# A decoder layer on one core: a gate row turned before its store, two compression layers in sequence, two heads' scores in one matmul

## The chip, the cores and the metric

The kernel runs on one core of a Trainium2 chip. The metric is the device time of one execution in microseconds. TensorE (PE) multiplies, VectorE (DVE) and ScalarE (ACT) work on elements, GpSimd (POOL) does a few powers and issues part of the DMAs, SyncE (SP) issues the weight loads.

## The reference, cut to what matters

One layer for 256 tokens of width 2048: a modulated norm, an input projection, two groups of attention heads, an output projection with gate 1, and then a product-key expert layer with gate 2. The modulation vectors are rows of `silu(c) @ w_ada + b_ada`. In the first group of heads, keys and values are also compressed: 32 tokens become one by a two-layer network, and the queries score the 15 compressed keys of their head group.

```python
def nsa_compress(k, pe, w1, w2, idx):
    ...
    out = jax.nn.gelu(blk @ w1) @ w2
...
Kc = nsa_compress(kc, pe_k, ck_w1, ck_w2, cmp_idx)
Vc = nsa_compress(vc, pe_v, cv_w1, cv_w2, cmp_idx)
...
s_c = jnp.einsum('bgrqd,bgnd->bgrqn', qi, Kc).astype(F32) * scale - slopes * d_c.astype(F32)
...
x = x + gate1 * (jnp.concatenate([o_nsa, o_ret], axis=-1) @ w_out[l])
```

## The kernel before, in words

The kernel has a front stage (everything up to the second norm, about the first 570 us) and an expert stage behind it, in which the expert tables u and v stream through TensorE. The change lies in the front, but for a call that is written differently.

Every weight block of the front arrives as a tile `raw` of 1 MB, in a ring of four buffers, issued by SP in program order. ACT casts it to `whi` and DVE forms the rest `wlo` (line 158, two halves per block, two buffers each); TensorE multiplies with both. Beside this stream run the 96 blocks of `w_ada` (`adaT`): DVE multiplies each with the row `crow` and sums it into one column of `modc` (line 198). The function `background` deals them out between the projection's blocks, `todo` holds their order: rows 1 and 0, then row 2 (gate 1), 4, 3 and 5 (gate 2).

A scheduler with a simulated timeline orders the instructions of each engine, except those that `keep_in_program_order` pins; each engine then works through its queue in that order. Tiles with the same tag share the buffers of a pool; in PSUM the tags A, S, T and O have two banks each.

The places that the change touches:

- Compression (lines 467 to 503). For keys, then values: DVE writes `blk` (one buffer) by eight additions, TensorE multiplies the 16 blocks of `w1` with it into `psc`, ACT takes the Gelu into `hid`. The second layer of the keys (`psk`, copied to `KcT`) stands ahead of the first layer of the values; then `hpad` and `psv` give the values in block-diagonal form (`BD`).
- Attention. For each of two pairs of head groups (`gp`), window and selected scores `sc` are formed, with exponentials `pr`, transposes `pT` and products `po`; between them the pairs of the projection's second half (`d_pair`, tile `psD`) and of the retention's values (`n_tile`, tile `psN`) run. At the end of each `gp`, the compressed scores `scc` (line 570) are formed, for each half `hf` of the 128 partitions by itself, as a query tile's 64 rows times 15 keys.
- Gate 1 (lines 200 to 209). `gate_store(2)` writes `modc[:, 2, :]`, 128 partitions of 16 numbers, as a row of 2048 numbers to DRAM, on POOL's queue. `row_load` reads the row back into all 128 partitions (1 MB) as `g1`. The output projection's first tile is multiplied with it (`xg`, line 716).
- Gate 2's row was already turned on TensorE and stored as 16 rows of 128 numbers, written out in place.

Of the kernel before, what the change touches and what calls it, by code (L numbers as in the profile page):

```python
# [9 lines left out]
F32 = mybir.dt.float32  # L10
# [6 lines left out]
AF = mybir.ActivationFunctionType  # L17
# [3 lines left out]
P = 128  # L21
S = 256
D = 2048
KB = D // P
# [3 lines left out]
NCMP = 15  # L28
# [87 lines left out]
def body(ctx, tc, a, out, dbg=None, stop=None):  # L116
    nc = tc.nc
# [3 lines left out]
    def dump(name, ap):  # L121
        if name in dbg:
            nc.sync.dma_start(dbg[name], ap)
# [47 lines left out]
    dram = ctx.enter_context(tc.tile_pool(name="dram", bufs=1, space=bass.MemoryType.DRAM))  # L171
# [5 lines left out]
    modc = base.tile([P, 6, KB], F32, name="modc")  # L177
# [19 lines left out]
        r = load(a["adaT"][j, k])  # L197
        nc.vector.scalar_tensor_tensor(r, r, 1.0, crow, op0=OP.mult, op1=OP.mult, accum_out=modc[:, j, k:k + 1])  # L198

    def gate_store(j):  # L200

        row = dram.tile([1, D], F32, name=f"row{j}")
        with nc.allow_non_contiguous_dma(reason="one row of 2048 numbers"):
            nc.gpsimd.dma_start(row.rearrange("o (k p) -> p (o k)", p=P), modc[:, j, :])
        return row

    def row_load(dst, row):

        nc.gpsimd.dma_start(dst, bass.AP(tensor=row.tensor, offset=row.offset, ap=[[0, P], [1, D]]))
# [68 lines left out]
    with ExitStack() as fctx:  # L278
        strm.append((fctx.enter_context(tc.tile_pool(name="strm", bufs=1)), dict(raw=4, whi=2, wlo=2)))
        fp = fctx.enter_context(tc.tile_pool(name="front", bufs=1))  # L280
# [28 lines left out]
        pp = fctx.enter_context(tc.tile_pool(name="fpsum", bufs=2, space=PS))  # L309
# [83 lines left out]
        for k in range(KB):  # L393
# [43 lines left out]
        qts = [xT[:, i, :] for i in range(8)]  # L437
# [27 lines left out]
        gate4 = gate.rearrange("p t (h b) -> p t h b", b=3)  # L465


        KcT = fp.tile([P, 4, NCMP], F32, name="KcT")
        BD = fp.tile([P, 4, 4, 64], F32, name="BD")
        nc.gpsimd.memset(BD, 0.0)  # L470
        pad = fp.tile([P, 4, 4, 32], F32, name="hpad", tag="tmp2", bufs=3)
        nc.gpsimd.memset(pad, 0.0)
        for kv in range(2):
            w1 = load(a["cw1"][kv].rearrange("p k e -> p (k e)"))
            psc = pp.tile([P, 4, NCMP], F32, name="psc", tag="S")
            view = kT2[:, 2 * kv:2 * kv + 2].rearrange("p a h (n e) -> p e (a h) n", e=8)
            blk = fp.tile([P, 16, 4, NCMP], F32, name="blk", bufs=1)
            for q in range(2):
                pe = csm[:, kv * 16 + 8 * q:kv * 16 + 8 * q + 8]
                for g in range(4):  # L480
                    nc.vector.tensor_add(blk[:, 8 * q:8 * q + 8, g, :], view[:, :, g, q:q + NCMP],
                                         pe[:, :, None].to_broadcast([P, 8, NCMP]))
            for pb in range(16):
                nc.tensor.matmul(psc, w1[:, pb * P:(pb + 1) * P], blk[:, pb], start=pb == 0, stop=pb == 15)
            hid = fp.tile([P, 4, NCMP], F32, name="hid", bufs=2)
            nc.scalar.activation(hid, psc, AF.Gelu_apprx_tanh)
            if kv == 0:
                w2 = csm[:, 32:96]
                psk = pp.tile([P, 4, NCMP], F32, name="psk", tag="S")
                w2d = fp.tile([P, 2, 64], F32, name="w2d")  # L490
                nc.vector.tensor_copy(w2d[:, 0, :], w2)
                nc.vector.tensor_copy(w2d[:, 1, :], w2)
                nc.tensor.matmul(psk, w2d.rearrange("p a d -> p (a d)"), hid, start=True, stop=True)
                nc.vector.tensor_copy(KcT, psk)
            else:
                for r in range(4):
                    nc.vector.tensor_copy(pad[:, :, r, 0:NCMP], hid)
                psv = pp.tile([P, 4, 64], F32, name="psv", tag="S")
                for g in range(4):
                    nc.tensor.matmul(psv[:, g, :], pad[:, g].rearrange("p r n -> p (r n)"), csm[:, 96:160],  # L500
                                     start=True, stop=True)
                for r in range(4):
                    nc.vector.tensor_copy(BD[32 * r:32 * r + 32, :, r, :], psv[32 * r:32 * r + 32, :, :])
        dump("KcT", KcT)
        dump("BD", BD)
        dump("gate", gate)

# [10 lines left out]
        for gp in range(2):  # L518
            o = fp.tile([P, 2, 8, 64], F32, name="onsa", bufs=1)
            ppad = fp.tile([P, 2, 8, 32], F32, name=f"ppad{gp}")  # L520
            nc.gpsimd.memset(ppad, 0.0)
            for r in range(4):
# [5 lines left out]
                for hf in range(2):  # L528
                    g = 2 * gp + hf
                    h = 4 * g + r  # L530
                    hs = slice(hf * 64, hf * 64 + 64)
# [30 lines left out]
                for hf in range(2):  # L562
                    nc.vector.tensor_add(o[:, :, hf * 4 + r, :], tmp[:, hf, :, 0, :], tmp[:, hf, :, 1, :])

            scs = [pp.tile([P, 2, 4, 16], F32, name="scc", tag="S") for _ in range(2)]
            for hf in range(2):
                hs = slice(hf * 64, hf * 64 + 64)
                for r in range(4):
                    for tt in range(2):
                        nc.tensor.matmul(scs[hf][:, tt, r, 0:NCMP], qts[gp * 4 + r][hs, tt * 128:(tt + 1) * 128],  # L570
                                         KcT[hs, 2 * gp + hf, :], start=True, stop=True)
            pv = ppad[:, :, :, 0:NCMP]
            den = fp.tile([P, 2, 8], F32, name="denc", bufs=1)
            mx = fp.tile([P, 2, 8], F32, name="mxc", bufs=1)
            bc = lambda x: x[:, :, None].to_broadcast([P, 8, NCMP])
            for tt in range(2):
                for hf in range(2):
                    nc.vector.tensor_add(pv[:, tt, 4 * hf:4 * hf + 4], scs[hf][:, tt, :, 0:NCMP],
                                         ncmp[:, tt, 8 * gp + 4 * hf:8 * gp + 4 * hf + 4, :])
                nc.vector.tensor_reduce(mx[:, tt, :], pv[:, tt], axis=AX.X, op=OP.min)  # L580
                nc.vector.tensor_sub(pv[:, tt], pv[:, tt], bc(mx[:, tt, :]))
                nc.scalar.activation(pv[:, tt], pv[:, tt], AF.Exp, scale=-1.0)
                nc.vector.reduce_sum(den[:, tt, :], pv[:, tt], axis=AX.X)
                nc.vector.tensor_mul(pv[:, tt], pv[:, tt], cval[:, tt, None, :].to_broadcast([P, 8, NCMP]))
# [19 lines left out]
            of = o.rearrange("p t h d -> p (t h) d")  # L604
# [96 lines left out]
        g1 = None  # L701
        x2d = dram.tile([P, 2, D], F32, name="x2d")
        for q in range(4):
            sl = slice(q * 512, (q + 1) * 512)
            ps = n_tile(q, "woutN", "AS"[q % 2], "out")
            if q == 0:
                while any(j == 2 for j, _ in todo):
                    background(1)
                g1 = fp.tile([P, D], F32, name="g1", tag="cT")
                row_load(g1, gate_store(2))  # L710
            if q == 3:
                background(len(todo))
            with tc.high_priority(offset=100 if q == 3 else 0):
                for tt in range(2):
                    t = fp.tile([P, 512], F32, name="xg", tag="tmp2", bufs=3)
                    nc.vector.tensor_mul(t, ps[tt], g1[:, sl])
                    nc.vector.tensor_add(x2[:, tt, sl], x2[:, tt, sl], t)
                    sq = fp.tile([P, 512], F32, name="sq2", tag="tmp2", bufs=3)
                    nc.scalar.activation(sq, x2[:, tt, sl], AF.Square, accum_out=ss[:, tt, q:q + 1])
                    nc.gpsimd.dma_start(x2d[:, tt, sl], x2[:, tt, sl])  # L720
# [23 lines left out]
    with ExitStack() as gctx:  # L744
        strm.append((gctx.enter_context(tc.tile_pool(name="strm2", bufs=1, reuse_waits="tile")), dict(raw=5, whi=3, wlo=2)))
        gp_ = gctx.enter_context(tc.tile_pool(name="peer", bufs=1, reuse_waits="tile"))
        ident = gp_.tile([P, P], F32, name="ident2")
# [387 lines left out]
        for i in range(16):  # L1135
            ps = first[i] if i < 2 else t_block(up, wq(i), bank("A"), dst=early if i == 2 else None)
# [134 lines left out]

        nc.vector.tensor_add(modc[:, 5, :], modc[:, 5, :], b_col[:, 5, :])
        nc.vector.tensor_scalar(modc[:, 5, :], modc[:, 5, :], 1.0 / GSC, None, op0=OP.mult)
        ps = up.tile([P, 512], F32, name="psh", tag=bank("S"))
        nc.tensor.transpose(ps[0:KB, 0:P], modc[:, 5, :], ident)
        r5 = gp_.tile([KB, P], F32, name="row5t", tag="ge", bufs=3)
        nc.scalar.copy(r5, ps[0:KB, 0:P])
        row5 = dram.tile([1, D], F32, name="row5")
        nc.gpsimd.dma_start(row5.rearrange("o (k p) -> (o k) p", p=P), r5)
        for _ in range(2):  # L1280
            x_tile(gp_)

# [13 lines left out]
def build(tc, a, out, dbg=None):  # L1296
    with ExitStack() as ctx:
        body(ctx, tc, a, out, dbg)
# [17 lines left out]
```

## Time and profile before

| | |
|---|---|
| median of 3 runs | 1890.0 us (1884.99 to 1891.03) |
| the profiled execution | 1895.85 us, its span 1894.1 us |
| PE busy | 1816.1 us, 96% |
| DVE busy | 1479.9 us, 78% |
| DMA moved | 652.93 MB, mean 345 GB/s |
| matmuls of `psN` (L452) | 172.8 us with whi, 104.4 us with wlo |

Busy time is summed over the whole span; a busy PE can still be slow, since short matmuls and a lowered clock count as busy. Times in rows of the timeline are microseconds from the span's start: start, duration, engine, line, operation, then in brackets how long the engine stood idle and for what. One fp32 matmul appears as two records in the profile.

### The profile page before, as it was taken

To read this page: it belongs to the slowest core of one execution; us is meant where nothing else is said; L and a number is where in the kernel's file an instruction comes from. 1 tells how busy PE (TensorE), PEld (TensorE's weight loads), DVE (VectorE), ACT (ScalarE), POOL (GpSimd) and SP (SyncE) were. 2 spreads that over 40 slices of the span, in tenths; PEclk is the share of its full clock that TensorE was granted. 3 is DMA by queue.
4 is the path that set the end of the run, shared out by engine and by line. 5 is a ranking of instruction groups with operands and counts; after the bars stand their busy time and mean duration, and the time that the engine had idled before them with its cause. 6 is when DMAs were issued, how large, how long until landed. Compare 5 with 4: busy or idle time off the path is not lost.

```text
span 1894.1 us, 28604 instructions
## 1 busy us (share of the span) xinstructions
PE 1816.1 (96%) x11303; PEld 1589.3 (84%) x11303; DVE 1479.9 (78%) x2333; ACT 708.7 (37%) x1279; POOL 379.5 (20%) x256
## 2 busy tenths in 40 slices
PE   5899999999997999999999999999999999999995
PEld 4899878788786899999997777779999997777773
DVE  7988877879788998778388999974455559888875
ACT  3444453625434422011035545541111114555552
POOL 1000001002001002111124444421111125544210
PEclk9999899989998999999999999999999999999998
DMA  8989876879887979999889999989989979999981
GB/s 350 388 323 373 309 274 231 311 258 349 298 321 276 339 278 342 424 395 355 356 320 406 422 417 413 416 337 425 367 330 355 366 301 421 422 413 387 383 294 45
DMA packets 94473, 652.93 MB, mean 345 GB/s; under 512 B 11409, under 2 KB 11617, under 8 KB 18433
## 3 DMA queue, kind: packets, MB, share of 16 engines
q1 hardware_dynamic: 66818, 467.78, 64.2%
q0 software_dynamic: 27520, 183.32, 24.2%
q8 instruction: 89, 1.46, 0.3%
q14 instruction: 46, 0.38, 0.1%
HBM read 644.97 MB, written 4.22 MB: 343 GB/s over the span
## 4 chain that ended last, share of the span: by engine, by line
PE 84%; DVE 9%; DMA 3%; issue 2%; ACT 1%; POOL 0%; SPq 0%; ACTq 0%; POOLq 0%; DVEq 0%
PE acc L964 31%; PE psU L1062 28%; PE psN L452 8%; PE psD L353 3%; DMA raw<-in_adaT 2%; PE bkB L353 2%; PE psA L236 2%; DVE raw L198 2%; DVE wlo L158 2%; PE pg L1047 1%; PE bkC L353 1%; PE bvB L405 1%; PE psA L237 1%; DMA raw<-in_winA 1%; PE pT L548 1%
## 5 line engine op out<-in xcount | busy, mean ns | idle before, releaser
L1062 PE MATMUL psU<-xT,raw 128*128 128x160 f32 x4096 | 569.9, 300 | 0.0
L1062 PEld LDWEIGHTS psU<-xT,raw 128*128 128x128 f32 x4096 | 558.3, 190 | 0.5
L964 PE MATMUL acc<-whi,cc 128*128 128x512 f32 x1512 | 367.8, 391 | 0.0
L964 PEld LDWEIGHTS acc<-whi,cc 128*128 128x128 f32 x1512 | 283.8, 188 | 68.9
L947 DVE TENSOR_TENSOR wlo<-raw,whi 128x2048 fp32r<-128x2048 f32 x126 | 288.2, 2288 | 63.6 <-issue 58.5
L964 PE MATMUL acc<-wlo,cc 128*128 128x512 f32 x1008 | 252.5, 391 | 0.6 <-DVE wlo L947 0.6
L946 ACT CAST whi<-raw 128x2048 fp32r<-128x2048 f32 x126 | 240.7, 1911 | 6.5 <-DMA raw<-in_v 6.5
L157 ACT CAST whi<-raw 128x1024 fp32r<-128x1024 f32 (+1 forms) x174 | 168.5, 1018 | 187.3 <-PE psN L452 43.8
L198 DVE SCALAR_TENSOR_TENSOR raw<-raw,crow 128x2048 f32<-128x2048 f32 x96 | 219.2, 2284 | 23.3 <-DMA raw<-in_adaT 23.2
L158 DVE TENSOR_TENSOR wlo<-raw,whi 128x1024 fp32r<-128x1024 f32 (+1 forms) x174 | 200.9, 1181 | 30.8 <-ACT whi L157 28.2
L964 PEld LDWEIGHTS acc<-wlo,cc 128*128 128x128 f32 x1008 | 162.0, 161 | 61.6 <-DVE wlo L947 1.3
L452 PE MATMUL psN<-whi,act 128*128 128x512 f32 x512 | 172.8, 414 | 1.3 <-ACT whi L157 1.1
L1068 DVE TENSOR_TENSOR X<-X,ge 128x160 f32<-128x160 f32 (+19 forms) x94 | 25.8, 276 | 165.3 <-ACT ge L1067 158.0
L1064 ACT ACTIVATE X<-psU 128x160 f32<-128x160 f32 (+19 forms) x102 | 25.6, 253 | 306.3 <-PE psU L1062 298.3
L452 PEld LDWEIGHTS psN<-whi,act 128*128 128x128 f32 x512 | 97.7, 194 | 26.9 <-issue 3.0
L452 PE MATMUL psN<-wlo,act 128*128 128x512 f32 x256 | 104.4, 410 | 3.6 <-DVE wlo L158 3.6
L941 ACT CAST cc<-X 128x192 fp32r<-128x192 f32 x128 | 44.8, 353 | 157.0 <-PE acc L964 155.9
L236 PE MATMUL psA<-act,whi 128*128 128x512 f32 x240 | 87.9, 407 | 3.2 <-ACT whi L157 3.2
L803 POOL DMA_INDIRECT rows<-in_urow,sx x32 | 71.8, 2244 | 91.6 <-DVE rows L844 76.3
L803 POOL DMA_INDIRECT s<-in_urow,sx x26 | 57.5, 2213 | 134.6 <-DVE s L844 101.9
L803 POOL DMA_INDIRECT xT<-in_v,sx x21 | 60.7, 2889 | 93.0 <-DVE cc L942 63.2
L844 DVE SCALAR_TENSOR_TENSOR rows<-rows,h2t 128x2048 f32<-128x2048 f32 x32 | 73.1, 2286 | 3.5 <-DMA rows<-in_urow,sx 3.5
(350 smaller groups left out, 2550.9 us busy)
## 6 DMA issues: line engine op xcount, KB each, us to landing
raw<-in_u SPq DMA_DIRECT2D x128, 1024.0 KB
raw<-in_v SPq DMA_DIRECT2D x128, 1024.0 KB
raw<-in_adaT SPq DMA_DIRECT2D x96, 1024.0 KB
raw<-in_winN SPq DMA_DIRECT2D x16, 1024.0 KB
raw<-in_woutN SPq DMA_DIRECT2D x16, 1024.0 KB
raw<-in_wqT SPq DMA_DIRECT2D x16, 1024.0 KB
raw<-in_winB SPq DMA_DIRECT2D x16, 832.0 KB
raw<-in_winD SPq DMA_DIRECT2D x12, 1024.0 KB
```

What stands on the lines that cost most here:

```text
L157: nc.scalar.copy(hi[:, sl], r[:, sl])
L158: nc.vector.tensor_sub(lo[:, sl], r[:, sl], hi[:, sl].bitcast(F32))
L198: nc.vector.scalar_tensor_tensor(r, r, 1.0, crow, op0=OP.mult, op1=OP.mult, accum_out=modc[:, j, k:k + 1])
L236: nc.tensor.matmul(p_, hi[:, sl], act[:, k], start=k == 0, stop=False, skip_group_check=True)
L353: nc.tensor.matmul(bank[:, b, :], x[:, w], y[:, k, :], start=k == k0 and n == 0 and first, stop=k == k1 - 1 and n == 2, skip_group_check=True)
L452: nc.tensor.matmul(ps[tt], x[:, k, ts_], y[:, w], start=k == 0 and j == 0, stop=k == KB - 1 and j == 2)
L803: pin(nc.gpsimd.indirect_dma_start(out=r, out_offset=None, in_=src, in_offset=bass.IndirectOffsetOnAxis(ap=o, axis=0)))
L844: pin(nc.vector.scalar_tensor_tensor(r, r, 1.0, h, op0=OP.mult, op1=OP.mult, accum_out=d[:, e:e + 1]))
L946: inorder(nc.scalar.copy(hi, r))
L947: nc.vector.tensor_sub(lo, r, hi.bitcast(F32))
L964: nc.tensor.matmul(acc[c][0:m], x, w[:, c[1] * 512:(c[1] + 1) * 512], start=jj == 0 and n == 0, stop=jj == HALF - 1 and n == 2 - c[0], ski ...
L1062: nc.tensor.matmul(ps, w[:, k * P:(k + 1) * P], xT[:, k, 0:TU], start=k == 0, stop=k == KB - 1)
```

## The change

Three edits. `gate_store` now takes a PSUM tile and a small SBUF tile: TensorE transposes the 16 columns of `modc`, ACT copies the result, and POOL stores 16 rows of 128 numbers; gate 2 calls the same function. In the compression both first layers are formed before the key's second layer, and the last matmul of the values' first layer and the key's second layer are pinned in that order. The compressed keys are kept as `Kc`, with 32 columns per pair of head groups: the first 16 hold one group's keys in the upper 64 partitions, the last 16 the other group's in the lower 64, and zeros elsewhere. One matmul over all 128 partitions so gives the scores of both halves.

```diff
-    def gate_store(j):
+    def gate_store(j, ps, ident, t):
         row = dram.tile([1, D], F32, name=f"row{j}")
-        with nc.allow_non_contiguous_dma(reason="one row of 2048 numbers"):
-            nc.gpsimd.dma_start(row.rearrange("o (k p) -> p (o k)", p=P), modc[:, j, :])
+        nc.tensor.transpose(ps, modc[:, j, :], ident)
+        nc.scalar.copy(t, ps)
+        nc.gpsimd.dma_start(row.rearrange("o (k p) -> (o k) p", p=P), t)
         return row
...
-        KcT = fp.tile([P, 4, NCMP], F32, name="KcT")
+        Kc = fp.tile([P, 2, 2, 16], F32, name="Kc")
+        nc.gpsimd.memset(Kc, 0.0)
...
             for pb in range(16):
-                nc.tensor.matmul(psc, w1[:, pb * P:(pb + 1) * P], blk[:, pb], start=pb == 0, stop=pb == 15)
-            hid = fp.tile([P, 4, NCMP], F32, name="hid", bufs=2)
-            nc.scalar.activation(hid, psc, AF.Gelu_apprx_tanh)
-            if kv == 0:
-                ...
-                nc.tensor.matmul(psk, w2d.rearrange("p a d -> p (a d)"), hid, start=True, stop=True)
-                nc.vector.tensor_copy(KcT, psk)
-            else:
-                ...
+                i = nc.tensor.matmul(psc, w1[:, pb * P:(pb + 1) * P], blk[:, pb], start=pb == 0, stop=pb == 15)
+            hids.append(fp.tile([P, 4, NCMP], F32, name="hid", bufs=2))
+            nc.scalar.activation(hids[-1], psc, AF.Gelu_apprx_tanh)
+        tc.keep_in_program_order(i)
...
+        tc.keep_in_program_order(nc.tensor.matmul(psk, w2d.rearrange("p a d -> p (a d)"), hids[0], start=True, stop=True))
+        for gp in range(2):
+            for hf in range(2):
+                hs = slice(hf * 64, hf * 64 + 64)
+                nc.vector.tensor_copy(Kc[hs, gp, hf, 0:NCMP], psk[hs, 2 * gp + hf, :])
...
-            scs = [pp.tile([P, 2, 4, 16], F32, name="scc", tag="S") for _ in range(2)]
-            for hf in range(2):
-                hs = slice(hf * 64, hf * 64 + 64)
-                for r in range(4):
-                    for tt in range(2):
-                        nc.tensor.matmul(scs[hf][:, tt, r, 0:NCMP], qts[gp * 4 + r][hs, tt * 128:(tt + 1) * 128],
-                                         KcT[hs, 2 * gp + hf, :], start=True, stop=True)
+            scs = pp.tile([P, 2, 4, 2, 16], F32, name="scc", tag="S")
+            for r in range(4):
+                for tt in range(2):
+                    nc.tensor.matmul(scs[:, tt, r].rearrange("p h n -> p (h n)"), qts[gp * 4 + r][:, tt * 128:(tt + 1) * 128],
+                                     Kc[:, gp].rearrange("p h n -> p (h n)"), start=True, stop=True)
...
-                row_load(g1, gate_store(2))
+                row_load(g1, gate_store(2, pp.tile([P, P], F32, name="psg1", tag="T")[0:KB, :], ident,
+                                        fp.tile([KB, P], F32, name="row2t")))
...
-        ps = up.tile([P, 512], F32, name="psh", tag=bank("S"))
-        nc.tensor.transpose(ps[0:KB, 0:P], modc[:, 5, :], ident)
-        ...
-        nc.gpsimd.dma_start(row5.rearrange("o (k p) -> (o k) p", p=P), r5)
+        row5 = gate_store(5, up.tile([P, 512], F32, name="psh", tag=bank("S"))[0:KB, 0:P], ident,
+                          gp_.tile([KB, P], F32, name="row5t", tag="ge", bufs=3))
```

The scheduler re-deals the neighbours of these instructions. On TensorE at the compression, before (the line numbers of the changed kernel are a few higher than those of the kernel before):

```order
L353 MATMUL psD<-act,wlo 128x256
L484 MATMUL psc<-blk,raw 128x60 x16
L353 MATMUL psD<-act,whi 128x256 x2
L493 MATMUL psk<-hid,w2d 128x60
L484 MATMUL psc<-blk,raw 128x60 x16
```

and in the changed kernel:

```order
L354 MATMUL psD<-act,wlo 128x256
L487 MATMUL psc<-blk,raw 128x60 x16
L354 MATMUL psD<-act,whi 128x256 x2
L487 MATMUL psc<-blk,raw 128x60 x16
L496 MATMUL psk<-hid,w2d 128x60
```

The second run of `psc` has moved ahead of `psk`.

On POOL's queue, before, with `row` the stored gate row, `g` the loaded one, `nal` and `dec` masks, `msn` and `brs` powers for norms, `x2d` the stored result:

```order
L533 DMA nal<-in_nali 128x384 x9
L204 DMA row_4435<-modc 128x16x1
L220 TENSOR_TENSOR msn<-msn,mhalf 128x16
L533 DMA nal<-in_nali 128x384 x3
L642 DMA dec<-in_dec 128x384 x8
L220 TENSOR_TENSOR msn<-msn,mhalf 128x16
L220 TENSOR_TENSOR brs<-brs,mhalf 128x2 x2
L209 DMA g_4434<-row_4435 128x2048
L220 TENSOR_TENSOR brs<-brs,mhalf 128x2 x6
L720 DMA x2d<-xT 128x512 x8
```

and in the changed kernel:

```order
L537 DMA nal<-in_nali 128x384 x9
L221 TENSOR_TENSOR msn<-msn,mhalf 128x16
L537 DMA nal<-in_nali 128x384 x3
L644 DMA dec<-in_dec 128x384 x8
L221 TENSOR_TENSOR msn<-msn,mhalf 128x16
L221 TENSOR_TENSOR brs<-brs,mhalf 128x2 x8
L205 DMA row_4423<-row2t 16x128
L210 DMA g_4420<-row_4423 128x2048
L723 DMA x2d<-xT 128x512 x8
```

Store and load have both moved behind the last `brs`, one directly behind the other.

On DVE, where the loaded row is first used (`xg`), with `wlo` the splits for the next weight blocks and `modc` the adaT sums, before:

```order
L198 SCALAR_TENSOR_TENSOR raw,modc<-raw,crow 128x2048
L676 TENSOR_TENSOR act<-oT,act 128x256
L716 TENSOR_TENSOR xg<-psN,g_4434 128x512
L717 TENSOR_TENSOR xT<-xT,xg 128x512
L158 TENSOR_TENSOR wlo<-raw,whi 128x1024
L716 TENSOR_TENSOR xg<-psN,g_4434 128x512
L158 TENSOR_TENSOR wlo<-raw,whi 128x1024
```

and in the changed kernel:

```order
L678 TENSOR_TENSOR act<-oT,act 128x256
L198 SCALAR_TENSOR_TENSOR raw,modc<-raw,crow 128x2048
L158 TENSOR_TENSOR wlo<-raw,whi 128x1024 x3
L719 TENSOR_TENSOR xg<-psN,g_4420 128x512
L158 TENSOR_TENSOR wlo<-raw,whi 128x1024
L720 TENSOR_TENSOR xT<-xT,xg 128x512
L719 TENSOR_TENSOR xg<-psN,g_4420 128x512
L720 TENSOR_TENSOR xT<-xT,xg 128x512
L198 SCALAR_TENSOR_TENSOR raw,modc<-raw,crow 128x2048
```

Three halves of `wlo` now stand ahead of the first `xg`, and one between the two.

More of the change, by code (lines that the diff above doesn't have):

```diff
@@ L472, in body @@
         nc.gpsimd.memset(pad, 0.0)
+        hids = []
         for kv in range(2):
@@ L483, in body @@
             for pb in range(16):
-                nc.tensor.matmul(psc, w1[:, pb * P:(pb + 1) * P], blk[:, pb], start=pb == 0, stop=pb == 15)
-            hid = fp.tile([P, 4, NCMP], F32, name="hid", bufs=2)
-            nc.scalar.activation(hid, psc, AF.Gelu_apprx_tanh)
-            if kv == 0:
[L488 to L493, printed above, removed]
-                nc.vector.tensor_copy(KcT, psk)
-            else:
-                for r in range(4):
[L497 to L503, printed above, removed]
@@ L504, in body @@
-        dump("KcT", KcT)
+                i = nc.tensor.matmul(psc, w1[:, pb * P:(pb + 1) * P], blk[:, pb], start=pb == 0, stop=pb == 15)
+            hids.append(fp.tile([P, 4, NCMP], F32, name="hid", bufs=2))
+            nc.scalar.activation(hids[-1], psc, AF.Gelu_apprx_tanh)
+        tc.keep_in_program_order(i)
+        w2 = csm[:, 32:96]
+        psk = pp.tile([P, 4, NCMP], F32, name="psk", tag="S")
+        w2d = fp.tile([P, 2, 64], F32, name="w2d")
+        nc.vector.tensor_copy(w2d[:, 0, :], w2)
@@ new lines, in body @@
+        nc.vector.tensor_copy(w2d[:, 1, :], w2)
+        tc.keep_in_program_order(nc.tensor.matmul(psk, w2d.rearrange("p a d -> p (a d)"), hids[0], start=True, stop=True))
[4 more added lines that the diff above has]
+        for r in range(4):
+            nc.vector.tensor_copy(pad[:, :, r, 0:NCMP], hids[1])
+        psv = pp.tile([P, 4, 64], F32, name="psv", tag="S")
@@ L505, in body @@
+        for g in range(4):
+            nc.tensor.matmul(psv[:, g, :], pad[:, g].rearrange("p r n -> p (r n)"), csm[:, 96:160],
+                             start=True, stop=True)
+        for r in range(4):
+            nc.vector.tensor_copy(BD[32 * r:32 * r + 32, :, r, :], psv[32 * r:32 * r + 32, :, :])
         dump("BD", BD)
@@ L563, in body @@
                     nc.vector.tensor_add(o[:, :, hf * 4 + r, :], tmp[:, hf, :, 0, :], tmp[:, hf, :, 1, :])
-            scs = [pp.tile([P, 2, 4, 16], F32, name="scc", tag="S") for _ in range(2)]
-            for hf in range(2):
-                hs = slice(hf * 64, hf * 64 + 64)
-                for r in range(4):
-                    for tt in range(2):
-                        nc.tensor.matmul(scs[hf][:, tt, r, 0:NCMP], qts[gp * 4 + r][hs, tt * 128:(tt + 1) * 128],
-                                         KcT[hs, 2 * gp + hf, :], start=True, stop=True)
+            scs = pp.tile([P, 2, 4, 2, 16], F32, name="scc", tag="S")
+            for r in range(4):
+                for tt in range(2):
+                    nc.tensor.matmul(scs[:, tt, r].rearrange("p h n -> p (h n)"), qts[gp * 4 + r][:, tt * 128:(tt + 1) * 128],
+                                     Kc[:, gp].rearrange("p h n -> p (h n)"), start=True, stop=True)
             pv = ppad[:, :, :, 0:NCMP]
@@ L577, in body @@
                 for hf in range(2):
-                    nc.vector.tensor_add(pv[:, tt, 4 * hf:4 * hf + 4], scs[hf][:, tt, :, 0:NCMP],
+                    nc.vector.tensor_add(pv[:, tt, 4 * hf:4 * hf + 4], scs[:, tt, :, hf, 0:NCMP],
                                          ncmp[:, tt, 8 * gp + 4 * hf:8 * gp + 4 * hf + 4, :])
@@ L1273, in body @@
         nc.vector.tensor_scalar(modc[:, 5, :], modc[:, 5, :], 1.0 / GSC, None, op0=OP.mult)
-        ps = up.tile([P, 512], F32, name="psh", tag=bank("S"))
-        nc.tensor.transpose(ps[0:KB, 0:P], modc[:, 5, :], ident)
-        r5 = gp_.tile([KB, P], F32, name="row5t", tag="ge", bufs=3)
-        nc.scalar.copy(r5, ps[0:KB, 0:P])
-        row5 = dram.tile([1, D], F32, name="row5")
-        nc.gpsimd.dma_start(row5.rearrange("o (k p) -> (o k) p", p=P), r5)
+        row5 = gate_store(5, up.tile([P, 512], F32, name="psh", tag=bank("S"))[0:KB, 0:P], ident,
+                          gp_.tile([KB, P], F32, name="row5t", tag="ge", bufs=3))
         for _ in range(2):
```

## The prediction

> **What bounds the kernel now.** I read the page first (busy shares and slices), then the windows of the front stage, then the timeline of each place that the change touches.
>
> ```profile
> PE 1816.1 (96%) x11303; PEld 1589.3 (84%) x11303; DVE 1479.9 (78%) x2333; ACT 708.7 (37%) x1279; POOL 379.5 (20%) x256
> PEclk9999899989998999999999999999999999999998
> DMA  8989876879887979999889999989989979999981
> ```
>
> TensorE (PE) is busy nearly throughout. From slice 12 on, where the expert layer runs, it stands at full clock; the change adds nothing there beyond re-ordered neighbours. All three edits lie in slices 4 to 11 (190 to 570 us), where the clock dips and the DMA share sags. The windows show where:
>
> ```profile
> core 0: us, PE busy (x) PEld busy (x) DVE busy (x) ACT busy (x) POOL busy (x), PEclk, DMA share, GB/s
> 200.00:210.00 10.00, 7.49 (x36) 7.29 (x36) 8.47 (x15) 4.79 (x6) 0.00 (x0) 0.60 0.91 342
> 300.00:310.00 10.00, 5.47 (x38) 5.27 (x38) 6.27 (x7) 2.11 (x3) 0.00 (x0) 0.89 0.29 96
> 380.00:390.00 10.00, 10.00 (x36) 8.22 (x35) 5.40 (x11) 1.74 (x6) 0.54 (x1) 0.50 0.72 243
> 450.00:460.00 10.00, 7.95 (x30) 6.02 (x29) 7.29 (x12) 5.62 (x10) 1.51 (x1) 0.90 1.01 390
> ```
>
> No engine and no DMA is full over this stretch: it is a chain of hand-overs, so time taken from the link that ends last there is time gained, until another link is late. The four rows are the four places of the sum.
>
> **First layers together (the stretch at 200).** Timeline, then one-microsecond windows:
>
> ```profile
> 196.06 3.78 PE L484 MATMUL psc<-blk,raw 128*128 128x60 f32 x32 [0.31 <-DVE blk L481]
> 199.87 0.50 PE L353 MATMUL psD<-act,whi 128*128 128x256 f32 x2
> 199.87 2.33 DVE L481 TENSOR_TENSOR blk<-kT,csm 128x120 f32<-128x120 f32 x8 [0.52 <-PE psc L484]
> 202.88 0.69 PE L493 MATMUL psk<-hid,w2d 128*128 128x60 f32 x2 [2.51 <-ACT hid L486]
> 203.36 7.04 PE L484 MATMUL psc<-blk,raw 128*128 128x60 f32 x32
> 210.40 5.87 PE psD L353 x29
> 217.95 4.45 PE psD L353 x36
> 201.00:202.00 1.00, 0.00 (x0) 0.00 (x0) 1.00 (x5) 0.98 (x2) 0.00 (x0) 0.97 1.05 442
> 202.00:203.00 1.00, 0.12 (x1) 0.12 (x1) 1.00 (x2) 0.82 (x2) 0.00 (x0) 0.50 1.02 426
> 214.00:215.00 1.00, 1.00 (x6) 1.00 (x6) 1.00 (x1) 0.00 (x0) 0.00 (x0) 0.50 1.02 418
> ```
>
> PE waits 2.51 us for the Gelu of the first layer, the granted clock falls to 0.50 at 202, and the second layer's 32 matmuls take 7.04 us where the first 32 took 3.78; the 29 psD behind them take 5.87 us, at 4.45/36 = 0.124 us each (full clock) they would take 3.6. Now the second first-layer follows the two psD directly. It still waits for its input: blk has one buffer, four of the eight additions (half of 2.33 us) end at 201.0, so PE idles about 0.7 us instead of 2.51. If that short gap keeps the clock up, the gain is 1.8 (wait) + 3.3 (7.04 - 3.78) + 2.3 (5.87 - 3.6) = 7.4 us; psk then finds its Gelu done. Bounds: 0 (the clock falls all the same and the next psD weights are late) to -7.4. I take -6, near the upper end, because the row at 199.87 shows the input ready early.
>
> The Trainium skill ("TensorE: Matmul & The Clock Gate", section "What's actually happening") says that the clock is halved after an idle window of some 3.4 us and released after a busy one of that length. This trace differs: the gap of 2.51 us was enough, and 7 us of back-to-back narrow matmuls did not release it. By that rule the order would not touch the clock, term one would be -1.8 and the forecast some 3 us higher.
>
> **Compressed scores of two heads in one matmul.**
>
> ```profile
> 271.66 1.38 PE L570 MATMUL scc<-KcT,xT 64*128 64x15 f32 x11
> 388.90 2.74 PE L570 MATMUL scc<-KcT,xT 64*128 64x15 f32 x12
> ```
>
> Per head group 32 matmul records (16 matmuls, two records each) become 16. A record costs 1.38/11 = 0.12 us at full clock and 2.74/12 = 0.22 at half (the 380:390 row). Sixteen fewer save 1.9 us in group 0 and 3.5 in group 1, where PE is 10.00 of 10 busy, so both count: -5.4. The new 32-column moving side was never run; the 60-column psc above costs 3.78/32 = 0.12 per record, so width up to there is free. Bounds: 0 (DVE or DMA is next) to -12, if the shorter low-work stretch also keeps the clock up: at full clock the ten microseconds of that row would take about 5, and the 0.50 stretch may last longer than the row. I take -5.4, crediting no clock. DVE's additions read one score tile instead of two; one PSUM bank of the two is then free for the window scores. The four Kc copies replace one 0.23 us copy, +0.6 us of DVE at a place where the 200:210 row leaves it 1.5 us free, 0 on the path; the memset of Kc on POOL lies among the others at the start, with POOL 20% busy.
>
> **Gate row stored as 16 rows.** The old store writes 2048 single numbers:
>
> ```profile
> L204 POOL DMA_DIRECT2D row<-modc x1: 1192/1192/1192, 290.8 to 290.8; - x1
> DMA to landing us min/median/max: 12.6/12.6/12.6
> 281.00 4.79 DMA raw<-in_adaT
> 291.69 11.95 DMA raw<-in_adaT
> 303.73 2.29 DVE L198 SCALAR_TENSOR_TENSOR raw<-raw,crow 128x2048 f32<-128x2048 f32 x1 [7.09 <-DMA raw<-in_adaT]
> 307.23 0.39 PE L353 MATMUL psD<-act,wlo 128*128 128x256 f32 x1 [4.53 <-DVE wlo L158]
> ```
>
> While it is in flight (290.8 to 303.4), a 1 MB adaT load takes 11.95 us, against 4.79 just before, and the queues move 96 GB/s in the 300:310 row. DVE stands in order behind that load for 7.09 us, and wlo behind DVE makes PE wait 4.53. Without the burst the load lands 7.1 us earlier, before PE runs dry. Bounds 0 to -7.1; I take PE's own wait, -4.5.
>
> **Where the store goes instead.** The turn takes the PSUM tag of the last head transposes, so it and the store stand behind them, and the 1 MB row load, which was issued at 444, now comes after the store. On POOL's queue both now follow all eight brs powers and precede the x2d stores, which need xg anyway. The turn itself only needs modc, ready long before, and holds PE for one transpose.
>
> ```profile
> 442.50 10.19 DMA raw<-in_adaT
> 456.88 0.50 PE L452 MATMUL psN<-wlo,act 128*128 128x512 f32 x1 [2.06 <-DVE wlo L158]
> 444.37 0.58 POOL L209 DMA_DIRECT2D g<-row  x1 [14.23 <-DVE xT L429]
> DMA to landing us min/median/max: 8.7/10.7/12.7
> 499.87 0.38 PE L512 MATMUL psT<-small,orr 128*128 128x128 f32 x2
> 501.97 0.47 ACT L515 ACTIVATE oT<-psT,cols 128x256 f32<-128x256 f32 x1
> sx<-gt POOLq DMA_DIRECT2D x1, 16.0 KB, 4.1
> 509.03 0.69 DVE L716 TENSOR_TENSOR xg<-psN,g 128x512 f32<-128x512 f32 x1 [2.97 <-PE psN L452]
> 511.63 56.65 PE psN L452 x235
> 515.45 1.22 DVE L158 TENSOR_TENSOR wlo<-raw,whi 128x1024 fp32r<-128x1024 f32 x1
> ```
>
> Leaving 444: the adaT load beside it took 10.19 us and PE waited 2.06 us; -2.1 (0 to -2.1). Arriving at 503: last psT 499.9, ACT's oT until 502.4, the copy 0.3, the store's issue 0.5 and landing 4.1 (the 16 KB row; the size is twice the store's) gives 507.3; the load's issue 0.6 and 8.7 to 12.7 us (two samples) give 516.6 to 520.6, for a first use (xg) that was ready at 509.03. DVE then stands 7.6 to 11.6 us in xg. Queued behind it on DVE: the rest of the wlo splits, which PE needs. Ahead of xg the new order keeps three wlo halves, 36 matmuls at 56.65/235 = 0.241 = 8.7 us, so PE runs to about 517.6. The next half comes 0.7 + 1.2 us after the row: PE waits 0.9 to 4.9 us, and again about 2.6 us for the half behind two xT, one xg, one adaT sum (2.3) and one split (1.2), less its 2.9 us of work. That is +3.5 to +7.5, with the row already there 0; I take +4.7. From there to 568 PE is the bound (235 matmuls without a stop), so it stays. The transpose and copy add 0.3.
>
> Sum: -6 - 5.4 - 4.5 - 2.1 + 4.7 + 0.3 = -13.0. The scheduler has re-dealt DVE, ACT and PE between 200 and 570, and some gain will meet the next late link; I keep four fifths, -10.5. The profiled execution took 1895.85 us (span 1894.1), 5.85 above the median of 1890.0. From the median: 1879.5, forecast 1880.
>
> **Rivals.**
> 1. The gate row decides (slower). If the store lands late behind 1 MB loads (as adaT took 11.95 us behind a store), the row comes another 8 us later, at 524 to 528; PE then waits 11 to 15 us, and DVE's hold keeps raw buffers and so the DMA back. With half of the other terms kept (18/2 = 9) that ends at 1890 + 15 - 9 = 1896 and above. It decides from a PE wait of about 13 us, where the gains end. For it: a DVE queue in order. Against: DMA had room at that place. Chance 0.11.
> 2. The gains are absorbed: the 200:210 row has DMA at 0.91 and 450:460 at 1.01, so PE time freed becomes a wait for the next weight load. Only the store's -4.5, -2.1 and the scores' -1.9 survive, against +5: -3.5, 1887. Chance 0.22.
> 3. The clock stays low through the compression whatever the order (mechanism: narrow matmuls don't raise it), -1.8 instead of -6, four fifths of -8.8: 1883. Chance 0.13. The page named above comes to the same number by its own rule.
> 4. The clock also stays up behind the second head group: -7 more, 1873. Chance 0.17.
>
> **Numbers.** My forecast has the remaining 0.37. A measurement of this kernel tells about 0.3% (5.7 us) from no change, so faster is below 1884.3: the forecast, rival 4 and half of rival 3, which lies at that border: 0.37 + 0.17 + 0.07 = 0.61. Same holds rival 2 and the other half, 0.28; slower is rival 1, 0.11. The range runs from below rival 4 (1873, less 6 for what the give-back of a fifth may not take) to past rival 2: 1867 to 1893.
>
> **What would show it.** In the new profile: psc as two runs of 32 records of about 3.8 us with PEclk 1.00 at 200 to 216; scc 32 records in all; no adaT load of 12 us near 291 and a DMA share above 0.7 in 300:310; a DVE idle before the first xg ended by the row's DMA, of 7 to 12 us, and PE waiting for wlo behind it. I am wrong if that wait is over 13 us, or if PE waits for weight loads by as much as it gained.

## The result, and the profile after

| | before | after |
|---|---|---|
| median | 1889.11 us (1884.99 to 1891.03) | 1878.02 us (1875.69 to 1878.28) |
| ratio | 1 | 0.9942, 95% interval 0.9929 to 0.9955 |
| profiled execution, its span | 1895.85, 1894.1 us | 1875.69, 1873.8 us |
| PE busy | 1816.1 us | 1797.7 us |

The change made the kernel 11.1 us faster (0.6%); the forecast was 1880. The profile of before lies 7 us above its median and that of after 2 us below, so their difference of 20 us overstates the change; a second profile of the kernel before (span 1885.9 us, from the experiments) is used below beside the first.

The page of the kernel after, the rows of PE, clock and DMA:

```profile
PE 1797.7 (96%) x11272; PEld 1574.5 (84%) x11272; DVE 1480.3 (79%) x2336; ACT 707.3 (38%) x1280; POOL 371.6 (20%) x257
PEclk9999899999999999999999999999999999999997
DMA  8989887889888799999889999989999979999971
```

The clock row has one digit below 9 left ahead of its last, in slice 4 (187 to 234 us; slices are counted from 0, as in the prediction). A dip that lies across two slices doesn't show in such a row: at 550 to 570 us the windows give a clock of 0.66 in this kernel, as they give 0.70 and 0.67 at 570 to 590 us in the kernel before. The windows of the places of the sum:

```profile
200.00:210.00 10.00, 9.20 (x47) 8.86 (x47) 8.18 (x21) 5.14 (x8) 0.00 (x0) 0.62 0.95 329
300.00:310.00 10.00, 10.00 (x82) 9.53 (x82) 8.64 (x13) 4.76 (x6) 0.00 (x0) 1.00 0.58 212
380.00:390.00 10.00, 10.00 (x60) 8.77 (x59) 9.48 (x17) 3.57 (x6) 1.64 (x3) 1.00 0.78 280
```

At 300 PE is full where it had 5.47 of 10. At 380 the clock is 1.00 where it was 0.50. In the second profile of the kernel before these two were 6.54 and 0.78, so a part of both differences belongs to the one execution that the prediction read. At 200 the clock is down as before (0.62, before 0.60). The timeline of the compression, of the scores and of the late gate row:

```profile
196.53 3.78 PE L487 MATMUL psc<-blk,raw 128*128 128x60 f32 x32 [0.31 <-DVE blk L484]
200.34 0.50 PE L354 MATMUL psD<-act,whi 128*128 128x256 f32 x2
201.62 6.47 PE L487 MATMUL psc<-blk,raw 128*128 128x60 f32 x32 [0.78 <-DVE blk L484]
278.92 1.97 PE L572 MATMUL scc<-Kc,xT 128*128 128x32 f32 x16
375.45 1.97 PE L572 MATMUL scc<-Kc,xT 128*128 128x32 f32 x16
482.63 0.56 POOL L210 DMA_DIRECT2D g<-row  x1 [4.31 <-DMA row<-row2t]
485.98 2.29 DVE L198 SCALAR_TENSOR_TENSOR raw<-raw,crow 128x2048 f32<-128x2048 f32 x1 [6.18 <-DMA raw<-in_adaT]
489.47 0.79 PE L453 MATMUL psN<-wlo,act 128*128 128x512 f32 x1 [3.45 <-DVE wlo L158]
491.60 0.69 DVE L719 TENSOR_TENSOR xg<-psN,g 128x512 f32<-128x512 f32 x1
```

The gap in front of the second `psc` shrank to 0.78 us as foreseen, but its matmuls still take 6.47 us. A head group's scores are one run of 1.97 us. The first `xg` has no bracket: the gate row was there in time. What makes PE wait there is an adaT load ahead of `wlo` on DVE.

One row was in nobody's sum. It is the end of the program, among SP's waits, of before and of after:

```profile
SPq L1311 <- PEq L1311: 0.7, 2, 0.5
```

```profile
SPq L1310 <- PEq L1310: 4.8, 2, 4.3
```

The columns are the total, the number of times and the longest. SP stands in the closing handshake 4.3 us where it stood 0.5. The row names PE's sequencer, but in the trace's records the instruction that runs so long is a drain at the end of GpSimd's queue: 2.40 us before, 9.91 us after (two more follow, of under 0.1 us; it is called the last drain here). From its start to the end of the program it is 10.7 us, where it was 6.5. From the start of the last `acc` matmul to the end it is 34.4 us, where it was 30.2.

### The profile page after: what moved, and what is told of

The parts are those of the page before. It is cut to its first block, busy times and chain, and to the rows that moved or that the text cites. A ratio compares the mean times of both kernels' runs of the same rounds, so it can differ in the third digit from the quotient of the medians.

```text
span 1873.8 us, 28539 instructions
## 1 busy us (share of the span) xinstructions
PE 1797.7 (96%) x11272; PEld 1574.5 (84%) x11272; DVE 1480.3 (79%) x2336; ACT 707.3 (38%) x1280; POOL 371.6 (20%) x257
## 4 chain that ended last, share of the span: by engine, by line
PE 86%; DVE 8%; DMA 3%; issue 1%; ACT 1%; POOL 0%; SPq 0%; ACTq 0%; POOLq 0%; DVEq 0%
PE acc L967 31%; PE psU L1065 28%; PE psN L453 8%; PE psD L354 3%; PE psA L237 2%; PE bkB L354 2%; DMA raw<-in_adaT 2%; DVE raw L198 1%; DVE wlo L158 1%; PE pg L1050 1%; PE psA L238 1%; PE bkC L354 1%; PE bvB L406 1%; DMA raw<-in_winA 1%; PE pT L552 1%
## 5 line engine op out<-in xcount | busy, mean ns | idle before, releaser
L453 PE MATMUL psN<-whi,act 128*128 128x512 f32 x512 | 166.5, 401 | 1.4 <-ACT act L677 0.7
L806 POOL DMA_INDIRECT s<-in_urow,sx x26 | 52.9, 2033 | 138.7 <-DVE s L847 109.0
## 6 DMA issues: line engine op xcount, KB each, us to landing
raw<-in_v SPq DMA_DIRECT2D x128, 1024.0 KB, 10.2
```

What stands on the lines that cost most here:

```text
L453: nc.tensor.matmul(ps[tt], x[:, k, ts_], y[:, w], start=k == 0 and j == 0, stop=k == KB - 1 and j == 2)
L806: pin(nc.gpsimd.indirect_dma_start(out=r, out_offset=None, in_=src, in_offset=bass.IndirectOffsetOnAxis(ap=o, axis=0)))
```

## The experiments

**Each part alone, and the whole without each.** Times are compared by medians and by their ratio to the kernel before. The hunks are those of the change; the part that is left out keeps its old lines:

```diff
 gate:    -gate_store(2), 2048 single numbers     +transpose, copy, 16 rows; gate 2 by the same function
 order:   -psc, psk, psc                          +psc, psc, psk, pinned
 scores:  -KcT, 16 matmuls of 64 rows a pair      +Kc with zeros, 8 matmuls of 128 rows, one tile
```

The kernel before once more:

> The kernel before, unchanged, for a second profile: ratio 1.000 +- 0.002. Theory A (each edit removes its own wait): the half clock behind the second head group's compressed scores is a matter of the phase of the clock's window, and may be shorter or absent here; the waits at the compression (PE 2.5 us for hid) and at the scattered store (adaT load of about 12 us, PE wait of about 4.5 us) return. Theory B (the gain is the clock): the half clock near 380 us lasts 10 us or more again.

Gate alone:

> The kernel before with the gate edit alone. Theory A: -5 us (PE wait of 4.5 us at the store and 2.1 us at the old row load gone, some 1 to 2 us back at the output projection), ratio 0.997; no adaT load over 8 us near 290 us. Theory B (the clock carries the gain): -2 us or less, ratio 0.999. Theory C (the parts do not add, the scheduler's re-deal decides): anything between -11 and +3.

Order alone (the second layer still copied to `KcT`):

> The kernel before with the order of the compression layers alone (compressed keys as before). Theory A: -2 to -3 us, ratio 0.9985: the clock falls at the second first layer all the same, as in the profile after, so only the wait for the Gelu (1.8 us) and part of the slow psD go. Theory B: 0. Theory C: anything between -8 and +5.

Scores alone (`Kc` filled in the old order):

> The kernel before with the two-head scores alone. Theory A: -3 to -4 us, ratio 0.998: sixteen records of 0.12 us less in each of two places, the clock not counted. Theory B: -8 us or more, ratio 0.995, and a granted clock of 1.00 around the second head group's scores. Theory C: anything between -11 and +5.

Without the gate edit:

> The whole change but for the gate row, which is stored as 2048 single numbers as before. Theory I (order and scores remove the same late links, so together they give what the better one gives alone, about -14 us; the gate edit costs about 4 us, the longer end of the program): 1874 us, 4 below the whole change, the end of the program from the first row of the last acc group's start at 30.2 us again, instead of 34.4. Theory A (parts add up: -9.8 and -13.6): 1866 us. Rival (in the whole change the gate edit gains at the store what it loses elsewhere): 1878 us.

Without the order:

> Gate row and scores changed, compression in the old order. Theory I: scores alone (1875) plus the gate edit's 3 to 4 us, 1878.5 us, that is no slower than the whole change, the end of the program 34.4 us after the last acc. Theory A (parts add): -13.6 + 3.4, 1879 us. Rival (the compression's order is worth its 6 us beside the scores): 1884 us.

Without the scores:

> Gate row and order changed, the scores in the old form (32 matmuls of 64 rows per two head groups, KcT). Theory I: order alone (1880) plus 3 to 4 us, 1883.5 us, with the clock down again at 380 us. Theory A (parts add): -9.8 + 3.4, 1882.7 us. Rival (scores are worth only the 5.4 us of their matmuls beside the rest): 1883 us; the three agree here, and the run is for the clock's rows and the end of the program.

| kernel | median us | ratio (95%) | half clock 270 to 400, us | PE in 300:310 | PE waits for wlo in psN, us | front's end, us | last drain, us |
|---|---|---|---|---|---|---|---|
| before, again | 1887.54 | 0.9994 (0.9978 to 1.0011) | 17 | 6.54 | 2.5 | 565.6 | 2.40 |
| gate | 1892.84 | 1.0018 (1.0002 to 1.0034) | 17 | 9.13 | 7.7 | 570.9 | 9.91 |
| order | 1880.04 | 0.9948 (0.9931 to 0.9965) | 14 | 10.00 | 1.3 | 556.9 | 2.40 |
| scores | 1875.15 | 0.9928 (0.9903 to 0.9952) | 0 | 9.43 | 1.3 | 554.4 | 2.40 |
| order, scores | 1871.36 | 0.9906 (0.9889 to 0.9923) | 0 | 10.00 | 2.7 | 552.4 | 2.40 |
| gate, scores | 1883.82 | 0.9975 (0.9964 to 0.9987) | 0 | 10.00 | 5.0 | 557.7 | 9.91 |
| gate, order | 1890.33 | 1.0013 (1.0000 to 1.0025) | 3 | 10.00 | 10.7 | 564.2 | 9.91 |
| all three (after) | 1878.02 | 0.9942 (0.9929 to 0.9955) | 0 | 10.00 | 3.5 | 551.4 | 9.91 |

Half clock is worked out from the windows of ten microseconds: a granted clock of 0.83 means 3.4 us at half. The front's end is the start of the first `psX` in the one profile of each kernel; in the first profile of the kernel before it was 573.7, so single profiles can differ by 8 us there.

The unchanged kernel gave its time again, and the waits at the compression (1.8 us) and at the store (3.5 us) came back; the half clock around 380 lasted 6.8 us, not the 17.1 of the first profile, as theory A had it. Of the parts alone, the gate was to gain by theories A and B, and cost 3.4 us; the order gained 9.8, more than any theory named; the scores gained 13.6 with the clock at 1.00, so theory A's 3 to 4 us fell and theory B's 8 or more came.

The parts don't add: -9.8 (order), -13.6 (scores) and about +3.5 (gate) make -20, measured -11. (Differences are of medians, or of ratios where these are given; the intervals reach 2 to 5 us to either side.) Order and scores together give -18, not -23: theory A (1866) fell, and theory I's 1874 was 3 too high. The gate edit costs in any company: +3.4 (by its ratio to before), +10.3 beside order, +8.7 beside scores, +6.7 beside both. The rival that it gains at the store what it loses elsewhere (1878 without it) fell too. Without the order, the rival's 1884 was right and theory I's 1878.5 wrong: the order is worth 5.8 us beside the other two. Without the scores, all theories said 1883 and 1890.33 came, with the clock up at 380 against theory I, and the longest PE waits of all in the output projection. That kernel is 3.3 us behind the whole change at its last `psD` (423.2 against 419.9 us) and 12.9 behind at the front's end, and 7.2 us of this are PE's waits for `wlo` (10.7 against 3.5): most of what the scores seem to be worth beside the gate edit is lost behind the scores, around the load of the gate row. The gate edit beside both others, in turn, shows no cost in the front (551.4 against 552.4); its end is 4.2 us longer, and some 2.5 of its 6.7 us have no place. So the kernel without its gate edit is the better one: its interval lies below that of the whole change.

Why the store's gain vanishes is in the windows of the kernel with order and scores but the old store (issued at 287.5, landed 12.3 us later):

```profile
290.00:300.00 10.00, 10.00 (x67) 8.46 (x66) 9.69 (x17) 3.11 (x7) 0.00 (x0) 1.00 0.55 46
300.00:310.00 10.00, 10.00 (x82) 9.65 (x82) 6.65 (x8) 5.05 (x6) 0.00 (x0) 1.00 0.77 305
```

The queues move 46 GB/s during the burst, but DVE has 9.69 us of work and PE is full in both windows. The burst now lies beside work that needs no load. In the kernel before, DVE had only 2.35 us of work at 290 to 300, and PE ran dry behind it.

**The row turned early.**

```diff
+                    if j == 2:
+                        row2.append(gate_store(2, pp.tile([P, P], F32, name="psg1", tag="A")[0:KB, :], ident,
+                                               fp.tile([KB, P], F32, name="row2t")))
...
-                row_load(g1, gate_store(2, ...))
+                row_load(g1, row2[0])
```

> The whole change, but gate 1's row is turned and stored as soon as its 16 sums are done (in a PSUM buffer of tag A), so store and load stand on GpSimd's queue where they stood before. Theory I (the late row itself costs nothing in the whole change, the 1 MB row load beside adaT does, wherever it stands; the end stays long): 1876 to 1879 us, no verdict against the whole change, end 34.4 us after the last acc. Theory L (late row: store and load in the output projection cost 5 us there): 1873 us. Store lands in about 5 us in both, and no adaT load near 290 takes 12 us.

It took 1877.08 us, ratio 0.9939 (0.9921 to 0.9957), the same as after. The store stands at 310.1 us, the row load at 427.6, near its place without the gate edit (425.8), and PE waits 2.1 us for `wlo` in `psN`, not 3.5; theory L's 1873 didn't come. But the early turn has a price of its own, among PE's waits:

```profile
PE psD L358 <- ACT row2t L204: 2.0, 1, 2.0
```

PE stands 2.0 us for ACT's copy of the turned row and has 7.99 of 10 at 300:310, where the whole change has 10.00. So this run swaps one loss for another, and doesn't give the price of the late row by itself. The wait for `wlo` does so better: 3.45 us in the whole change, 2.72 without its gate edit, so less than a microsecond. Where the late row did hold PE, without the scores, the rows are these:

```profile
483.22 0.56 POOL L210 DMA_DIRECT2D g<-row  x1 [1.81 <-DMA row<-row2t]
484.13 0.33 SPq L148 DMA_DIRECT2D raw<-in_adaT  x1
493.57 2.29 DVE L198 SCALAR_TENSOR_TENSOR raw<-raw,crow 128x2048 f32<-128x2048 f32 x1 [9.13 <-DMA raw<-in_adaT]
497.06 0.79 PE L453 MATMUL psN<-wlo,act 128*128 128x512 f32 x1 [6.77 <-DVE wlo L158]
```

The adaT load, issued right behind the row load of the same size, came 9.4 us later; DVE stood for it and PE for the `wlo` behind it. DVE never stood for the gate row itself: in none of these kernels does an `xg` wait for its load.

**The same store twice, and the burst put back.** The first tests the program's end, the second the price of the burst.

```diff
+        if j == 2:
+            spare = dram.tile([1, D], F32, name="spare")
+            nc.gpsimd.dma_start(spare.rearrange("o (k p) -> (o k) p", p=P), t)
```

> The kernel with gate 1's row turned and stored early, and the same 16 rows stored once more to a spare row right behind, which no one reads. In ten profiles GpSimd's last instruction, a drain, took 2.40 us where the software queue had moved 27520 packets, and 9.91 us where it had moved 27504. Theory N (the number of packets decides, or their number by ring): 27520 again, drain 2.40, 1873 us. Theory K (the kind of store decides, since the scattered one is missing): drain 9.91 and 1877 us.

```diff
+                        spare = dram.tile([1, D], F32, name="spare")
+                        with nc.allow_non_contiguous_dma(reason="one row of 2048 numbers"):
+                            nc.gpsimd.dma_start(spare.rearrange("o (k p) -> p (o k)", p=P), modc[:, j, :])
```

> The kernel with gate 1's row stored early, and beside it the old store of 2048 single numbers to a spare row, which no one reads. Theory P (the prediction: the burst costs PE 4.5 to 7.1 us): 1882 us and PE dry at 300 to 310 us. Theory H (with the compression and the scores changed, the burst lies beside work that needs no load, as in the kernel with the old gate edit, where PE was 10.00 of 10 busy at 300 to 310): within 2 us of the kernel without the burst, 1877 us. If GpSimd's last drain is 2.40 us again (27536 packets), 4.2 us less in each.

With one store more, which no one reads, the kernel is faster: 1872.11 us, ratio 0.9912 (0.9893 to 0.9930), and its slowest run (1873.5) is faster than the fastest of the kernel with the row early alone (1874.3). The row of the software queue on its page (packets, MB, share), and SP's wait at the end:

```profile
q0 software_dynamic: 27536, 183.33, 24.6%
```

```profile
SPq L1316 <- PEq L1316: 0.7, 2, 0.5
```

The drain took 1.34 us. With the burst the kernel took 1872.27 us, ratio 0.9914 (0.9896 to 0.9932), with 27552 packets and a drain of 2.48. Over all profiles:

```text
packets on the software queue   GpSimd's last drain   kernels
27504                           9.91 us               gate; gate+scores; gate+order; after; row early
27520                           2.40 us               the seven with the old store alone
27536                           1.34 us               row early, stored twice
27552                           2.48 us               row early, and the burst
```

Theory K (the scattered store's absence lengthens the drain) is out, since an additional store of 16 rows shortens it. Theory N's 27520 was miscounted, a store of 16 rows being 32 packets; that the time hangs on the number of packets fits all 14 profiles, but four numbers don't tell how, and another property that goes with them isn't excluded. Only the 9.91 lengthens the program: from the drain's start to the end it is 6.5 us with 1.34, 2.40 and 2.48, and 10.7 with 9.91. The 4.2 us between them are real: -5.0 by the medians, though the front was 2.1 us slower (first `psX` at 550.7, not 548.6). The burst costs nothing here: PE has 7.99 of 10 at 300:310 with it and without it, by the wait for the turned row. Theory P's +4.5 to +7.1 is out, theory H with its 4.2 us less gave 1873.

**The score matmuls twice.** From the kernel with order and scores:

```diff
-                    nc.tensor.matmul(scs[:, tt, r]..., qts[gp * 4 + r]..., Kc[:, gp]..., start=True, stop=True)
+                    for _ in range(2):
+                        nc.tensor.matmul(scs[:, tt, r]..., qts[gp * 4 + r]..., Kc[:, gp]..., start=True, stop=True)
```

> Order and scores changed, the old gate store, and each of the 16 score matmuls of a head group issued twice, so 32 again, but from one moving tile into one PSUM tile. Theory M (the number of matmuls is what the change saves): 32 more records a group at 0.12 us, 1.9 us for each 16, +3.8 us, 1875 us, clock full at 380. Theory C (a long stretch of narrow matmuls lowers the clock, that is most of the gain): the granted clock falls to 0.5 again behind the score matmuls at 280 or 380 us, +7 or more, 1878 us and above. Theory T (one tile and one PSUM bank less is what counts): 1871 to 1873 us.

It took 1874.43 us, ratio 0.9928 (0.9909 to 0.9947), 3.1 above its base with intervals that overlap. The clock did fall, at the first head group:

```profile
280.00:290.00 10.00, 10.00 (x43) 8.88 (x42) 6.93 (x26) 1.96 (x7) 1.74 (x2) 0.50 0.83 302
290.00:300.00 10.00, 10.00 (x58) 8.25 (x57) 7.54 (x20) 3.33 (x13) 0.56 (x1) 0.82 0.32 56
```

```profile
277.63 3.27 PE L572 MATMUL scc<-Kc,xT 128*128 128x32 f32 x24
```

By windows of one microsecond it falls at 279.9 us, inside these 24 records, and PE was busy in every one of the ten microseconds before: here it fell with no gap at all. It stays at half for 13.6 us, as theory C foresaw, at theory M's price or less. The number of matmuls and the half clock that came with it explain some 3 us by the medians (the intervals allow more), and the front is no longer for it (551.7, base 552.4). So most of the scores' 8.7 us (beside order) probably comes from what this kernel keeps: one score tile and one PSUM bank instead of two. With order alone, the second head group's scores ran in pieces from 381.1 to 394.5 us, and DVE's second pair of additions waited 3.47 us for the last of them (before: 376.8 to 391.6, and 3.17 or, in the second profile, 0.32); after, they ran from 375.45 to 377.42, and DVE waited 0.74. How much of the rest is that and how much the new deal of the neighbours was not taken apart.

**A second buffer for the input of the compression.** From the kernel with order and scores:

```diff
-            blk = fp.tile([P, 16, 4, NCMP], F32, name="blk", bufs=1)
+            blk = fp.tile([P, 16, 4, NCMP], F32, name=f"blk{kv}", tag=("blk", "f4k")[kv], bufs=1 + kv)
```

> Order and scores changed, the old gate store, and a second buffer for blk, so that the second first layer need not wait for its input and follows the first one without a gap. Theory G (the gap of about 1 us in front of the second psc lowers the clock, as the prediction's condition had it): granted clock 1.00 throughout 200 to 216, the second psc about 3.8 us, psv some 3 us earlier, 1868 us. Theory N (narrow matmuls lower the clock whatever the gap): half clock for 7 us or more behind the first psc all the same, psv at most 1 us earlier, 1871 us.

The second buffer comes from the ring of `kcv`, `kT2` and `vr`; the two `psD` that stood between the first layers now stand elsewhere. Theory G is right on the clock. Timeline, and two of the one-microsecond windows:

```profile
196.90 7.25 PE L486 MATMUL psc<-blk,raw 128*128 128x60 f32 x64
207.59 1.00 PE L504 MATMUL psv<-csm,hpad 128*128 128x64 f32 x8
```

```profile
204.00:205.00 1.00, 1.00 (x11) 1.00 (x11) 0.55 (x4) 0.22 (x1) 0.00 (x0) 1.00 1.09 459
210.00:211.00 1.00, 1.00 (x10) 1.00 (x10) 0.97 (x2) 1.00 (x2) 0.00 (x0) 1.00 0.98 418
```

All 64 records run in 7.25 us at full clock, which stays up to 218, and `psv` starts at 207.6 instead of 213.8. Yet the kernel took 1881.32 us, ratio 0.9959 (0.9942 to 0.9975): 10 slower than its base, not 3 faster. The 6 us are gone by the first scores (277.1 us, base 277.8): by SP's rows in the timeline its weight loads lead the base's by 2.5 us at 234 and by 0.3 at 250. Then the burst, still in this kernel, is on the path again. The chain that ended last:

```profile
292.51 1.14 DVE wlo L158
293.74 2.22 DVE raw L198 x2
295.98 14.40 DMA raw<-in_adaT
```

```profile
310.00:320.00 10.00, 6.53 (x21) 4.74 (x19) 9.60 (x11) 2.52 (x3) 0.00 (x0) 0.66 0.95 356
```

An adaT load of 14.40 us stands in the chain behind the store issued at 292.8, and PE has 6.53 of 10, at a clock of 0.66. The last score matmul starts at 387.8, 10 us behind the base. The idle 3.5 us and the lowered clock are a part of these 10; where the rest was lost was not followed up.

## Why the prediction was right, and where its steps were not

The time (1880 against 1878.0) came out by terms that missed in opposite directions; so close a hit was luck. What each part is worth beside the other two is the difference between after and the kernel without it.

- **First layers together, -6.** Measured -5.8 beside the others, but not by the step named. The wait fell by 1.7 as computed; the second `psc` took 6.47 us, not 3.8, and the clock came back at about 212.5 instead of 215.6. The condition "if that short gap keeps the clock up" failed: with 0.78 us the clock was lost, and the one kernel without a gap kept it. So this term's 3.3 and 2.3 were mis-sized, and "PEclk 1.00 at 200 to 216" was wrong. Rival 3 had the outcome; for its mechanism (narrow matmuls) the evidence is split: 64 records of 60 columns ran at full clock, but inside 24 records of 32 columns it fell without a gap. What the order gained lies behind: alone it starts `psv` no earlier than the kernel before (214.8 us against 214.7 in the second profile; 216.1 in the first) but has PE full at 300:310, against 6.54.
- **Scores, -5.4.** Measured -12.3 beside the others, -8.7 to -13.6 in the rest. The step that failed is the kind of price: 16 records a group, put back by doubling them, were some 3 us, with a half clock on top. The 3.5 us for the second group also priced the sixteen records at half clock, where 12 of the group's 32 had run at full (from 376.75 us, 1.51 us). That 32 records remain was right. Rival 4 had the clock right (1.00 behind the second group), not its price: 13.6 us of half clock at 280 cost some 3 us with the added matmuls, and without the scores the clock was up at 380 and the kernel still 12.3 us behind. What makes up the rest of this term is open.
- **Scattered store, -4.5.** Measured 0 beside the other two, and PE has 9.43 (scores) and 10.00 (order) of 10 at 300:310 with the burst still there. The bound "0 to -7.1" held; taking PE's wait in the kernel before was wrong, because another part of the same change had covered it. Alone the gain exists at its place (PE 9.13 of 10 in that window against 6.54), though not in the time. In the whole change the DMA share there is 0.58, not above 0.7.
- **Late gate row, +4.7.** Its size was about right where it was alone (PE waits for `wlo` 7.7 us in `psN`, against 2.5), but by another mechanism: the row's 1 MB beside an adaT load, not DVE standing in `xg`. The row came in time: it landed 6.5 us after its issue, where the prediction had 8.7 to 12.7, and store and load were issued at 477.8 and 482.6, not at 503. In the whole change it cost less than a microsecond by that wait (3.45 us against 2.72 without the gate edit).
- **Leaving 444, -2.1.** Not shown: the wait of 2.06 us stands in the profile that the prediction read; in the second profile of the same kernel the longest wait of `psN` for `wlo` is 1.0 us.
- **The end of the program.** +4.2 us, in no step. A replaced DMA was priced at its place only.
- **Together.** The gate edit was put at -1.6 (-4.5 -2.1 +4.7 +0.3) and is +6.7; the scores were put at -5.4 and are -12.3. The two errors, 8.3 and 6.9, cancel but for 1.4. The fifth that was taken off for lost gains was too little if the parts alone are added (-20, measured -11) and about right for the sum as it stood.
- **The clock row.** The prediction read full clock "from slice 12 on". The digit of slice 12 is an 8, and the windows at 570 to 590 us give 0.70 and 0.67. No term of the sum used it.

## What to carry to other kernels

Run each part of a change alone and the whole without each: a part can cost time inside a change that gains. Here the change without its gate edit (1871.4 us), or with its row turned early and one store more (1872.1), beats both kernels; the second buffer together with the early row was not tried. Parts that each fill the same dry stretch (here 300 to 310 us) pay once, so the terms of a sum are to be priced in the company of the others. A gain is worth what is left of it at the next shared resource: here 6 us won at 208 were gone at 277, and the kernel ended slower.

## What the hardware showed

- The clock: in the middle of narrow matmuls (60 columns) a gap of PE of 0.78 us (after) and of 1.00 us (order and scores) came with a halving 0.7 and 1.8 us after PE had gone back to work (at 202.3 and 203.9), while the one kernel that ran the same 64 matmuls without a gap kept it. A gap is not needed, though: with the score matmuls doubled the clock fell at 279.9 us, inside 24 records of 32 columns, with PE busy all the time. What exactly is weighed, these runs don't settle. The stretches at half clock are multiples of about 3.4 us: 10.2 us in after, 6.8 with order and scores, 3.4 wherever a window of ten reads 0.83. The Trainium skill ("TensorE: Matmul & The Clock Gate", section "What's actually happening") gives a free-running window of that length. The multiples agree; that a whole window must be idle does not, since gaps of about 1 us, or none, were enough here.
- GpSimd's last drain: 2.40 us in seven profiles, 9.91 in five, to within 2 ns, and 1.34 and 2.48 in one each, going with the packets that its queue had moved, the changed store among them more than a millisecond before. At 9.91 it holds the end of the program (10.7 us from its start, else 6.5), and the waits put that under another engine's name.
- Beside one store of 2048 single numbers the queues moved 46 GB/s for ten microseconds (order and scores), and a 1 MB load took 11.95 us (before) and 14.40 (second buffer), against 4.79 just before the store. Whether PE stood for it differed: it had 5.47 of 10 at 300:310 in the kernel before and 10.00 with order and scores.
